# Splitting the weights of a hybrid decoder step: the low parts are computed on VectorE instead of GpSimd

## The chip, the cores and the metric

The kernel runs on one core of a Trainium2 chip. Five engines work side by side, each through its own queue in the order in which the program stands there: TensorE (PE in the profile) multiplies matrices, VectorE (DVE) and ScalarE (ACT) work elementwise and can read TensorE's results in PSUM, GpSimd (POOL) works elementwise on SBUF, and SyncE (SP) issues the DMAs. Semaphores make one engine wait for another. The metric is the device time of one execution in microseconds. The kernel before takes 4083.31 us (median of 3 runs, 4079.41 to 4086.87).

## The reference

One layer of a decoder is computed for a prompt of 2048 tokens and for 8 sample rows with a paged cache, all in float32, with a model width of 1024. Cut to what matters:

```python
h = rmsnorm(x, g_norm1) * (1 + sc1) + sh1            # sc, sh, ga: silu(c) @ w_ada + b_ada
qkv, z, beta, a, aq, ak, av, iq, ik, iw = split(h @ w_in)
o_gdn = gated_delta_rule(silu(conv(qkv)), beta, a)   # 4 heads, in chunks
o_att = sparse_attention(aq, ak, av, iq, ik, iw)     # scores, best 256 keys of each row, softmax
x = x + ga1 * (concat(o_gdn, o_att) @ w_out)
h2 = rmsnorm(x, g_norm2) * (1 + sc2) + sh2
gate, up = split(h2 @ w_ffn_in)                      # 2 x 2816 columns
x = x + ga2 * ((silu(gate) * up) @ w_ffn_out)
```

The sample rows go through the same layer with their own cache and state.

## The kernel before

The dense products keep float32 accuracy by splitting: an operand is rounded to a high part, and the rounding error is a low part. Each dense product is three matmuls (`mm3`, lines 157 to 159): high by high, high by low, low by high. Every tile of weights (128 x 512) is made by `weights`: a DMA brings the raw tile into `wr` (two buffers), ScalarE writes the high part into `wi` (line 141, `wi` has three buffers), and line 142 writes the low part, `wr` minus the high part, on GpSimd. 712 tiles are made so. The tiles of `w_in` are stored back to DRAM the first time and reloaded whole for later groups (line 135), so that they are split once. The kernel's activations are split in the same manner, with the low part on GpSimd (lines 361, 1362 and 1425).

The prompt is worked in four groups of 512 tokens. Stage one is, for each group, the projection (`project`, a convolution and a rotary step behind it) and the DeltaNet chunks (`chunks`, `state`), with the modulation products of `w_ada` (`modulate`) between them. GpSimd does much of a chunk: the squares and the normalising of q and k (lines 745 and 752), decays (774, 776), the start of the triangular inverse (792, 793), the square root by a power (190); in the projection it does the rotary step (610 to 613) and the low part of the index queries (690). Stage two is `groups`: for each group the sparse attention of the blocks of the next group (`index`, `select`, `attend`), then `ffn`: output projection, norm, and eleven pairs of feed-forward columns, two at a time, each followed by its part of the second product, whose result is added to the residual by a multiply on VectorE (line 1352) and an add on GpSimd (1353). VectorE carries the attention: it weights and sums the index scores (1241 to 1245), finds the 256 best keys by a bisection (`select`; line 1139 counts over the whole row, ten times a block), and takes the row maxima of the logits (1280). The sample rows' attention (`sample_steps`, with `sample_gdn` inside) stands in the program ahead of the third group's `ffn` (groups are counted from nought: `ffn(2)`), the schedule puts most of it at that `ffn`'s end, and the last group, `ffn(3)`, runs alone behind it.

No order is written by hand. The tile framework schedules the whole program by a model of the engines' times, and the static order of every queue is what that schedule gives; attention and feed-forward of stage two come out interleaved. Another engine for one line therefore changes the order on all queues.

Of the kernel before, what the change touches and what calls it, by code (L numbers as in the profile page):

```python
# [24 lines left out]
F32 = mybir.dt.float32  # L25
# [4 lines left out]
OP = mybir.AluOpType  # L30
# [77 lines left out]
class K:  # L108
# [21 lines left out]
    def weights(self, src, key=None):  # L130

        nc = self.nc
        w = self.wp.tile([128, 2, 512], F32R, name="wi", tag="wi", bufs=WI)
        if key in self.kept:
            nc.sync.dma_start(w.bitcast(F32), self.kept[key])
            return w[:, 0], w[:, 1]
        wr = self.wp.tile([128, 512], F32, name="wr", tag="wr", bufs=WR)
        n = 512 // len(src)
        for j, s in enumerate(src):
            nc.sync.dma_start(wr[:, j * n:(j + 1) * n], s)  # L140
        nc.scalar.copy(w[:, 0], wr)  # L141
        nc.gpsimd.tensor_tensor(w[:, 1], wr, w[:, 0].bitcast(F32), op=OP.subtract)  # L142
        if key is not None:
            self.kept[key] = self.dr.tile([128, 2, 512], F32, name="kept")
            nc.sync.dma_start(self.kept[key], w.bitcast(F32))
        return w[:, 0], w[:, 1]
# [1347 lines left out]
```

## Time and profile before

| | before |
|---|---|
| median of 3 runs | 4083.31 us |
| profiled execution | 4080.21 us, span 4078.1 us |
| TensorE busy | 3699.3 us (91%) |
| GpSimd busy | 1992.0 us (49%) |
| VectorE busy | 1873.0 us (46%) |
| ScalarE busy | 1357.3 us (33%) |
| granted TensorE clock, mean | 0.952 |

Busy time is the time in which an engine executes; a group of instructions is named by its line in the kernel, its engine, what it writes and what it reads. The waits say which instruction ended an idle time of the engine named first. A granted clock of 1.0 is 2.4 GHz.

### The profile page before, as it was taken

Reading aid. Unit: us, or ns where it says so; the run is one execution under the profiler, and the core shown is the slowest. Engines: PE = TensorE matmul, PEld = TensorE weight load, DVE = VectorE, ACT = ScalarE, POOL = GpSimd, SP = SyncE. Lnnn points to the kernel's source line nnn. Section 1 sums busy time; section 2 is a strip of 40 time slices with the busy share of each in tenths; the row PEclk is TensorE's granted clock in tenths of the full one; section 3 lists DMA queues with packets and bytes.
Section 4 is the critical chain, followed back from the end, with each engine's and each line's share of the span. In section 5 each row is a group of like instructions: output and inputs, shape, how many; then the busy total and the mean of one; then the engine's idle time right before and its main releaser. Section 6 shows DMA issues by size and latency. Waiting matters only on the chain. (4 is left out here: it accounts for less than half of the span.)

```text
span 4078.1 us, 51174 instructions
## 1 busy us (share of the span) xinstructions
PE 3699.3 (91%) x17420; PEld 2852.2 (70%) x17420; DVE 1873.0 (46%) x3492; ACT 1357.3 (33%) x2583; POOL 1992.0 (49%) x1897
## 2 busy tenths in 40 slices
PE   8888988899798879999998999998999996889997
PEld 4766877777686657677776777876877754467775
DVE  2423432441355223866668757387671238022123
ACT  2233223322332333333344443344433331132222
POOL 3366234432621575544564555564555552246555
PEclk9899999999899889999999999999999996989998
DMA  6653453373346334355535333234333333332222
GB/s 233 209 204 118 128 199 113 118 239 132 124 157 215 103 94 139 101 145 163 154 105 172 92 95 102 88 119 162 93 103 101 91 101 126 133 100 81 80 78 71
DMA packets 368313, 528.21 MB, mean 130 GB/s; under 512 B 45612, under 2 KB 246353, under 8 KB 365986
## 3 DMA queue, kind: packets, MB, share of 16 engines
q1 hardware_dynamic: 368042, 524.86, 40.5%
q8 instruction: 139, 2.28, 0.2%
q14 instruction: 132, 1.08, 0.1%
HBM read 427.33 MB, written 116.36 MB: 133 GB/s over the span
## 5 line engine op out<-in xcount | busy, mean ns | idle before, releaser
L142 POOL TENSOR_TENSOR wi<-wr,wi 128x512 fp32r<-128x512 f32 x712 | 937.6, 1323 | 1060.3 <-ACT wi L141 1030.7
L141 ACT CAST wi<-wr 128x512 fp32r<-128x512 f32 x712 | 439.5, 620 | 1118.7 <-PE d L159 345.6
L157 PE MATMUL d<-hh,wi 128*128 128x512 f32 x1792 | 736.0, 411 | 23.4 <-DVE tm L1352 7.0
L158 PE MATMUL d<-hl,wi 128*128 128x512 f32 x1792 | 717.2, 400 | 0.0
L159 PE MATMUL d<-hh,wi 128*128 128x512 f32 x1792 | 653.4, 403 | 0.0
L157 PEld LDWEIGHTS d<-hh,wi 128*128 128x128 f32 x1792 | 339.6, 190 | 118.9 <-DVE tm L1352 11.3
L159 PEld LDWEIGHTS d<-hh,wi 128*128 128x128 f32 x1792 | 338.3, 189 | 89.1 <-issue 6.7
L158 PEld LDWEIGHTS d<-hl,wi 128*128 128x128 f32 x1792 | 339.5, 189 | 77.5 <-issue 5.5
L1353 POOL TENSOR_TENSOR xt<-xt,tm 128x512 f32<-128x512 f32 x224 | 302.4, 1366 | 50.5 <-DVE tm L1352 34.3
L157 PE MATMUL d<-wi,hh 128*128 128x512 f32 x768 | 297.2, 411 | 24.5 <-DMA wi<-kept 15.5
L1245 DVE SCALAR_TENSOR_TENSOR sc<-rl,iw,sc 128x512 f32<-128x512 f32 (+3 forms) x224 | 222.2, 992 | 196.3 <-ACT rl L1238 187.4
L158 PE MATMUL d<-wi,hh 128*128 128x512 f32 x768 | 308.9, 402 | 0.2 <-POOL wi L142 0.2
L159 PE MATMUL d<-wi,hl 128*128 128x512 f32 x768 | 306.0, 400 | 0.0
L158 PE MATMUL d<-wi,ah 128*128 128x512 f32 x704 | 275.9, 395 | 0.9 <-POOL wi L142 0.9
L159 PE MATMUL d<-wi,al 128*128 128x512 f32 x704 | 271.4, 397 | 0.0
L157 PE MATMUL d<-wi,ah 128*128 128x512 f32 x704 | 256.5, 407 | 7.6 <-ACT ah L1424 3.6
L1352 DVE TENSOR_TENSOR tm<-d,row 128x512 f32<-128x512 f32 x224 | 150.1, 685 | 221.9 <-PE d L159 160.4
L1419 DVE SCALAR_TENSOR_TENSOR th<-th,d 128x512 f32<-128x512 f32 x88 | 58.1, 682 | 373.5 <-ACT th L1418 373.3
L806 DVE COPY_PREDICATED Dm<-cl,g 128x512 f32<-128x512 uint8 x96 | 70.0, 731 | 312.0 <-PE g L805 311.8
L1238 ACT ACTIVATE rl<-s 128x512 f32<-128x512 f32 (+3 forms) x288 | 148.1, 543 | 149.2 <-PE s L1236 110.4
L1139 DVE TENSOR_SCALAR_CACHE_REDUCE bias<-sc,sv 128x640 bf16<-128x640 f32 (+11 forms) x120 | 193.3, 1611 | 3.2
L157 PEld LDWEIGHTS d<-wi,hh 128*128 128x128 f32 x768 | 146.5, 192 | 66.4 <-DMA wi<-kept 17.8
(504 smaller groups left out, 6398.7 us busy)
## 6 DMA issues: line engine op xcount, KB each, us to landing
wr<-in_w_ffn_in_dram SPq DMA_DIRECT2D x704, 128.0 KB, 2.3
wi<-kept SPq DMA_DIRECT2D x168, 512.0 KB, 4.1
wr<-in_w_ffn_out_dram SPq DMA_DIRECT2D x176, 256.0 KB, 2.7
kept<-wi SPq DMA_DIRECT2D x56, 512.0 KB, 2.9
xt<-in_x_prompt_dram SPq DMA_DIRECT2D x8, 2048.0 KB, 7.6
wr<-in_w_ada_dram SPq DMA_DIRECT2D x64, 256.0 KB, 2.8
wr<-in_w_out_dram SPq DMA_DIRECT2D x64, 256.0 KB, 2.6
wr<-in_w_in_dram SPq DMA_DIRECT2D x56, 256.0 KB, 3.7
```

The lines of the kernel that those rows point to most:

```text
L141: nc.scalar.copy(w[:, 0], wr)
L142: nc.gpsimd.tensor_tensor(w[:, 1], wr, w[:, 0].bitcast(F32), op=OP.subtract)
L157: nc.tensor.matmul(out, wh, xh, start=start, stop=False, **kw)
L158: nc.tensor.matmul(out, wh, xl, start=False, stop=False, **kw)
L159: nc.tensor.matmul(out, wl, xh, start=False, stop=stop, **kw)
L806: nc.vector.copy_predicated(v4(Dm), self.cl[:, lv, :].unsqueeze(1).to_broadcast([128, H, 128]), v4(pp))
L1139: nc.vector.tensor_scalar(c, s, t, None, op0=OP.is_ge, op1=OP.add, accum_out=cnt)
L1238: nc.scalar.activation(r[:, :w], ps[:, :w], AF.Relu)
L1245: nc.vector.scalar_tensor_tensor(s, r[:, :w], iw, s, op0=OP.mult, op1=OP.add)
L1352: nc.vector.tensor_tensor(tm[:rows], pd[:rows], rw, op=OP.mult)
L1353: nc.gpsimd.tensor_tensor(xt, xt, tm[:rows], op=OP.add)
L1419: nc.vector.scalar_tensor_tensor(th, th, 1.0, pd[j], op0=OP.add, op1=OP.mult)
```

## The change

```diff
         nc.scalar.copy(w[:, 0], wr)
-        nc.gpsimd.tensor_tensor(w[:, 1], wr, w[:, 0].bitcast(F32), op=OP.subtract)
+        nc.vector.tensor_tensor(w[:, 1], wr, w[:, 0].bitcast(F32), op=OP.subtract)
```

The 712 subtractions of line 142 go from GpSimd's queue to VectorE's. Everything else computes what it did, where it did; its place in the queues is found anew by the scheduler. Three places show how.

GpSimd's queue where the last group's DeltaNet chunks meet the modulation products (`Y`, `S`, `kq`, `rnz`, `qk`, `qe` and `kd` belong to the chunks). Before:

```order
589 L855 TENSOR_TENSOR Y<-qe 128x512
590 L142 TENSOR_TENSOR wi<-wr,wi 128x512
591 L849 TENSOR_TENSOR S_169<-S_170,gc 128x512
592 L745 TENSOR_TENSOR kq<-qk 128x1024
593 L142 TENSOR_TENSOR wi<-wr,wi 128x512
594 L190 TENSOR_TENSOR r4z<-r4y,mhalf 128x4
595 L142 TENSOR_TENSOR wi<-wr,wi 128x512
596 L190 TENSOR_TENSOR rnz<-rny,mhalf 128x8
597 L859 TENSOR_TENSOR qe<-qe,r4z 128x512
598 L142 TENSOR_TENSOR wi<-wr,wi 128x512
599 L752 TENSOR_TENSOR qk<-qk,rnz 128x1024
```

The same place now:

```order
547 L855 TENSOR_TENSOR Y<-qe 128x512
548 L849 TENSOR_TENSOR S_169<-S_170,gc 128x512
549 L745 TENSOR_TENSOR kq<-qk 128x1024
550 L190 TENSOR_TENSOR r4z<-r4y,mhalf 128x4
551 L859 TENSOR_TENSOR qe<-qe,r4z 128x512
552 L190 TENSOR_TENSOR rnz<-rny,mhalf 128x8
553 L860 TENSOR_TENSOR qe<-qe,gzc 128x512
554 L752 TENSOR_TENSOR qk<-qk,rnz 128x1024
```

The chunks' own instructions follow each other, without a weight tile between them.

VectorE's queue in the bisection of a block of the second group (`bias` and `sv` are the mask and the small values of `select`, `big` the logits). Before:

```order
1213 L1139 TENSOR_SCALAR bias,sv<-sc,sv 128x1024
1214 L1140 TENSOR_SCALAR sv<-sv 128x1
1215 L1141 SCALAR_TENSOR_TENSOR sv<-sv,sW 128x1
1216 L1139 TENSOR_SCALAR bias,sv<-sc,sv 128x1024
1217 L1280 ISA big,st<-s,bias,st 128x384
1218 L1280 ISA st 128x1
1219 L1140 TENSOR_SCALAR sv<-sv 128x1
```

Now, in the bisection of the same block:

```order
1422 L1139 TENSOR_SCALAR bias,sv<-sc,sv 128x1024
1423 L1140 TENSOR_SCALAR sv<-sv 128x1
1424 L142 TENSOR_TENSOR wi<-wr,wi 128x512
1425 L1141 SCALAR_TENSOR_TENSOR sv<-sv,sW 128x1
1426 L1280 ISA big,st<-s,bias,st 128x384
1427 L1280 ISA st 128x1
1428 L1139 TENSOR_SCALAR bias,sv<-sc,sv 128x1024
```

A weight tile's low part now waits in one queue with the counts of the bisection and the logits' maxima.

TensorE's queue where the sample rows' attention follows `ffn(2)`: line 1035 transposes the paged index keys of one sample row, 1039 and 1041 score them, 908 opens `sample_gdn`. Before, the last two rows' steps and what stands behind them:

```order
9678 L159 MATMUL d<-wi,al 128x512
9679 L1039 MATMUL g<-big,iqTs 8x512
9680 L1322 MATMUL d<-cf,mod 128x128 x4
9681 L1039 MATMUL g<-big,iqTs 8x512
9682 L1322 MATMUL d<-cf,mod 128x128 x4
9683 L1041 MATMUL s<-big,oT 8x512
9684 L908 MATMUL g<-cf,big 128x24 x12
9685 L1333 MATMUL d<-cf,mod 8x128 x4
9686 L1041 MATMUL s<-big,oT 8x512
9687 L913 MATMUL g<-cf,raws 8x128 x8
9688 L1333 MATMUL d<-cf,mod 8x128 x4
9689 L157 MATMUL d<-wi,hh 128x512
```

Now the same place:

```order
9759 L1035 MATMUL g<-cf,PT 64x128 x4
9760 L1041 MATMUL s<-big,oT 8x512
9761 L1035 MATMUL g<-cf,PT 64x128 x4
9762 L1039 MATMUL g<-big,iqTs 8x512 x2
9763 L1041 MATMUL s<-big,oT 8x512
9764 L908 MATMUL g<-cf,big 128x24 x12
9765 L1041 MATMUL s<-big,oT 8x512
9766 L913 MATMUL g<-cf,raws 8x128 x12
9767 L929 MATMUL g<-rl,ones 128x64
```

Before, dense matmuls (line 157, the first of the last group's output projection) stand between and behind these steps; now the index steps of four and a half of the eight sample rows stand behind the last dense matmul, and `sample_gdn` follows them directly.

## Rows read from the trace of the kernel before

**Rows 1.** The page: busy time, share of the span and instructions of each engine.

```profile
PE 3699.3 (91%) x17420; PEld 2852.2 (70%) x17420; DVE 1873.0 (46%) x3492; ACT 1357.3 (33%) x2583; POOL 1992.0 (49%) x1897
```

**Rows 2.** Windows, four stages: start:end, length, busy us by engine, clock, DMA share, GB/s.

```profile
0.00:1561.00 1561.00, 1358.57 (x7253) 1090.64 (x7253) 556.42 (x1220) 473.37 (x951) 676.39 (x846) 0.93 0.48 157
1561.00:3105.00 1544.00, 1468.77 (x6449) 1145.52 (x6448) 1034.05 (x1806) 612.66 (x1132) 828.34 (x632) 0.98 0.40 123
3105.00:3540.00 435.00, 386.39 (x1633) 250.58 (x1632) 147.11 (x271) 118.20 (x209) 171.05 (x164) 0.90 0.35 113
3540.00:4078.10 538.10, 485.55 (x2091) 365.44 (x2089) 135.41 (x197) 153.11 (x292) 316.21 (x259) 0.96 0.27 82
```

**Rows 3.** The same windows for line 142 alone: GpSimd busy, clock, DMA share, GB/s.

```profile
0.00:1561.00 1561.00, 179.19 (x139) 0.93 0.48 157
1561.00:3105.00 1544.00, 495.11 (x369) 0.98 0.40 123
...
3540.00:4078.10 538.10, 182.83 (x143) 0.96 0.27 82
```

**Rows 4.** What TensorE waited for, whole run: us in total, times, longest.

```profile
PE d L694 <- POOL iqs L690: 27.0, 6, 6.8
PE d L174 <- POOL wi L142: 19.6, 15, 2.9
...
PE g L729 <- POOL qk L752: 16.4, 9, 5.1
...
PE g L729 <- POOL E L793: 9.1, 5, 4.8
```

**Rows 5.** Windows: a stretch of chunks with modulation products, all engines; columns as in Rows 2.

```profile
1423.00:1488.00 65.00, 41.62 (x192) 26.66 (x190) 18.42 (x44) 21.90 (x38) 59.88 (x50) 0.79 0.35 102
```

**Rows 6.** The same stretch, line 142 alone.

```profile
1423.00:1488.00 65.00, 26.04 (x22) 0.79 0.35 102
```

**Rows 7.** Groups of instructions, shapes apart: busy us, mean ns | idle before, releasers.

```profile
L142 POOL TENSOR_TENSOR wi<-wr,wi 128x512 fp32r<-128x512 f32 x712 | 937.6, 1323 | 1060.3 <-ACT wi L141 1030.7 <-DMA wr<-in_w_ffn_in_dram 7.8 <-DMA kept<-wi 5.8
...
L1245 DVE SCALAR_TENSOR_TENSOR sc<-rl,iw,sc 128x512 f32<-128x512 f32 x167 | 176.2, 1055 | 155.3 <-ACT rl L1238 149.2 <-ACT ah L1424 0.5
```

**Rows 8.** Lines 629, 1352 and 1245: duration ns min/median/max, first and last start, forms.

```profile
L629 DVE SCALAR_TENSOR_TENSOR cth<-cth,ca x48: 623/684/707, 100.8 to 1236.9; 128x512 f32<-128x512 f32 x48
...
L1352 DVE TENSOR_TENSOR tm<-d,row x224: 666/685/693, 1526.6 to 4053.6; 128x512 f32<-128x512 f32 x112
...
L1245 DVE SCALAR_TENSOR_TENSOR sc<-rl,iw,sc x224: 336/753/1868, 1630.6 to 2955.7; 128x512 f32<-128x512 f32 x85, 128x128 f32<-128x128 f32 x9, 128x256 f32<-128x256 f32 x9, 128x384 f32<-128x384 f32 x9
```

**Rows 9.** Windows of stage two, each about a pair of feed-forward steps; columns as in Rows 2.

```profile
1688.00:1781.00 93.00, 85.07 (x364) 66.99 (x363) 68.03 (x159) 33.92 (x66) 46.15 (x37) 0.95 0.40 113
...
2196.00:2328.00 132.00, 121.24 (x522) 90.59 (x521) 108.78 (x199) 56.24 (x107) 64.04 (x49) 0.97 0.39 123
...
2511.00:2599.00 88.00, 87.95 (x390) 70.15 (x390) 42.48 (x63) 36.08 (x63) 48.00 (x37) 1.00 0.31 93
...
2798.00:2930.00 132.00, 124.09 (x540) 94.88 (x541) 102.37 (x171) 57.90 (x108) 60.69 (x46) 0.96 0.38 120
2930.00:3021.00 91.00, 89.41 (x384) 69.63 (x383) 75.43 (x113) 32.23 (x53) 50.01 (x39) 1.00 0.31 91
```

**Rows 10.** Timeline of TensorE behind ffn(2): start us, us, instruction [idle before <-releaser].

```profile
3345.22 0.92 PE L908 MATMUL g<-cf,big 24*128 24x24 f32 x12
...
3359.04 0.40 PE L159 MATMUL d<-wi,hl 128*128 128x512 f32 x1
...
3432.00 1.09 PE L1064 MATMUL g<-cf,big 128*128 128x128 f32 x4 [2.44 <-DMA big<-kp_d]
```

**Rows 11.** Timeline of VectorE in the same stretch.

```profile
3361.67 4.85 DVE L1470 SCALAR_TENSOR_TENSOR xt<-xt,fin4z,row 128x1024 f32<-128x1024 f32 x4
```

**Rows 12.** The chain that ended last, at its end: start us, us, what.

```profile
4045.18 1.25 POOL wi L142
4046.44 1.26 POOL xt L1353
```

## Prediction

> **What bounds the kernel now.** I read the page's busy shares first [rows 1]: TensorE is busy 91% of the span, VectorE 46%, GpSimd 49%. The kernel is TensorE's as long as the others deliver in time; the change moves work between two engines that are half idle on the average. The average hides stages, so the next view is the table of windows. I cut the span into four stages [rows 2]: stage one (projections, DeltaNet chunks, modulation), stage two (feed-forward with the attention of the blocks to come), stage three (the end of ffn(2) and the sample rows), stage four (ffn(3) alone). In stage one TensorE is busy 1358.6 of 1561 us, 87%, with VectorE at 36% and GpSimd at 43%. In stage two it is at 95%, with VectorE at 67% and GpSimd at 54%. In stage three it is at 89%. In stage four it is at 90% as a whole, with VectorE at 25%; the loss lies at the ends of that stage. So stage one has VectorE to spare, and stage two is the place where VectorE is already the fuller of the two.
>
> The same windows for line 142 alone say where the moved work lies [rows 3]: 139 of the 712 subtractions in stage one (179.2 us of GpSimd), 369 in stage two (495.1 us), 143 in stage four (182.8 us), and by difference about 61 in stage three.
>
> The third view is the list of waits of TensorE [rows 4]. GpSimd ends 27.0 us of its waits with the index queries (line 690), 19.6 with line 142, 16.4 with the normalised q and k (752), 9.1 with the start of the inverse (793): 72 us, nearly all in stage one. The window 1423 to 1488 shows why [rows 5]: GpSimd is busy 59.9 of 65 us, TensorE only 41.6 at a granted clock of 0.79. Of the 59.9 us, 26.0 are line 142 [rows 6].
>
> **The change part by part.** 712 subtractions of 1323 ns each leave GpSimd, 937.6 us [rows 7]; GpSimd keeps 1054 us. VectorE gets 712 instructions that no row of before shows on it in this form. The nearest row is line 629, the same size with both inputs in SBUF: median 684 ns, at most 707 [rows 8]. The other end is line 1245, also two inputs in SBUF, which takes 1055 ns at this size in stage two [rows 7], with single ones up to 1868 ns, while line 1352, with one input from PSUM, never leaves 666 to 693 ns [rows 8]. The difference is company: line 1245 runs while GpSimd is 54% busy, and what is 128x512 from two SBUF inputs there costs 1055 - 684 = 371 ns more. So I bound one subtraction by 0.68 and 1.06 us. With line 142 gone GpSimd is busy (828.3 - 495.1) / 1544 = 22% of stage two. If the surcharge goes with GpSimd's share, it becomes 371 x 22/54 = 150 ns: I take 0.83 us for one subtraction, and line 1245 gains 0.22 us in each of its 224, 49 us.
>
> This has a rule behind it. The Trainium skill, page SBUF — State Buffer, section Who interferes with whom, says that a VectorE instruction with two SBUF inputs and a GpSimd instruction that reads SBUF exclude each other, and that the second to come waits for the whole of the first. The trace agrees: line 1245 against line 1352 above. It speaks against this change, since the subtraction keeps two SBUF inputs and only changes sides. By the rule a surcharge stays as long as GpSimd reads SBUF beside it, and the sum is the one below; without it a subtraction would take 0.68 us, line 1245 would lose its whole 371 ns (83 us), and VectorE would stand at (1034 + 252 - 83) / 1544 = 78% in stage two.
>
> Stage one. Line 142's own 19.6 us of TensorE's waits shrink to a third, since the queue is emptier and the instruction shorter: 13 us gained. The other 52.5 us are chains of GpSimd work in which line 142 has 179.2 of 676.4 us, 26%: 14 us gained. In the other direction 139 x 0.75 = 104 us come onto VectorE, which then stands at 42% of the stage; that cover is ample. I take -27 us; the bounds are 0, if other links of these chains are as late, and -72, if all these waits go. The order shows GpSimd's queue there without the tiles, so the relief itself is certain.
>
> Stage two. VectorE gets 369 x 0.83 = 306 us and loses 49: 1034 + 306 - 49 = 1291 of 1544 us, 84% instead of 67%, 17 points more in every window. In single windows [rows 9] that is 73 + 17 = 90% (from 1688), 82 + 17 = 99% (2196), 78 + 17 = 95% (2798), 83 + 17 = 100% (2930), but 48 + 17 = 65% (2511). Cut at the pairs of feed-forward steps, stage two has fifteen such windows, and nine of them, 985 us together, have VectorE at 67% or more now, 75% on the average, with TensorE busy 933 us of them, 95%. Rows 9 show how TensorE fares with VectorE's load: 99.9% at 48, and 91 to 98% at 73 to 83. An engine that works in order at 92% or more can't be on time for each tile. What waits: a subtraction now stands behind counts of the bisection and logits' maxima, and waits for ScalarE's high part, as GpSimd did for 1030.7 us in all [rows 7]; behind it the attention's next instructions stand, and TensorE needs both, the tile for the feed-forward and the scores' sums for the attention. The cover is two finished tiles ahead. I take 90% for TensorE in the nine windows: 933 / 0.90 = 1037, which is 52 us more. The bounds: 0, if the schedule's interleaving holds and the cover is enough; and with 1.06 us each and no gain for line 1245 the load grows by 25 points to 100% in the nine windows, and with a tenth of the time lost between instructions they take 985 / 0.90 = 1094, which is 110 us more.
>
> Stage three. The schedule, which sees a fuller VectorE, moves the attention back against the feed-forward; in TensorE's order the index steps of four and a half of the eight sample rows now stand behind the last dense matmul. Before, `sample_gdn` begins at 3345.22 and the dense matmuls run on to 3359.04 beside it [rows 10]: these 13.8 us of the chain to the paged keys (3432.00) are no longer covered. The four final scalings of 4.85 us that stand in that chain on VectorE [rows 11] now stand ahead of it: -5. The sample steps themselves are TensorE's work that was done elsewhere before, but alone each waits about 1 us for ScalarE: +4. The sum is +13; the bounds are -5 (only the scalings count) and +35 (the steps take 5 us each and nothing comes back).
>
> Stage four. VectorE goes from 25% to (135.4 + 143 x 0.83) / 538 = 47%, which is still cover for every tile. Off the last chain goes one subtraction of 1.25 us that stood between two adds on GpSimd [rows 12]: -2, between 0 and -8.
>
> The sum: -27 + 52 + 13 - 2 = +36 us on the profiled execution's 4080.2 us, 4116. That execution lies 3 us below the median of the runs, so I forecast 4119 us.
>
> **The rivals.** *GpSimd's relief decides (faster).* In stage two the schedule knows the new load and has put the subtractions between the counts one by one; if no tile comes more than two tiles late, TensorE keeps its 95% and the 52 us are nought. It decides from the point at which stage two and three together lose less than the 27 us of stage one. With -45 in stage one (half-way to its bound), +5 in stage three and -2 in stage four it is -42: 4041. For it: VectorE has 16% left in stage two and much more elsewhere, and at 83% (window 2930) TensorE was still busy 98%. Against it: no window of before has VectorE over 83%, and four would have it at 90% or more among those shown. The Trainium skill, page GPSIMD Engine Reference, section 4.1 Engine selection, sends elementwise work on two inputs to VectorE as the faster engine; by that rule the 4041 would be the outcome, and rows 7 and 8 agree as to the single instruction, 1323 against 684 ns.
>
> *The two cancel (no change).* Stage one's gain and stage two's loss are both a few tens of us from bounds that include 0; with -27, +20, +10 and -2 the time stays: 4084. For it: TensorE has 91% of the span already. Against it: it needs two unlike sizes to meet.
>
> *The exclusion costs full price (much slower).* If each subtraction meets an instruction of GpSimd as line 1245 did, it takes 1.06 us and GpSimd's adds are held as well: +110 in stage two, +13, and -15 in stage one: +108, 4191. For it: single ones of 1868 ns. Against it: GpSimd is 22% busy then, not 54%.
>
> **How the numbers follow.** The forecast 0.50, with 4090 to 4155 as its own range; GpSimd's relief 0.24; no change 0.13; full price 0.13. I count as no change what lies within 0.2% (8 us), about what a measurement of this kernel can tell. Slower: 0.50 + 0.13 = 0.63; same 0.13; faster 0.24. The range 4045 to 4185 leaves out about half of the relief's chance and half of the full price's.
>
> **What would show it.** In the profile after, GpSimd should stand near 1050 us and VectorE near 1873 + 712 x 0.83 - 49 = 2415 us. Line 142 on VectorE should take 0.75 to 0.9 us on the mean, line 1245 at 128x512 about 0.83. Stage one should end some 27 us earlier, with the waits for lines 690, 752 and 142 smaller; stage two should be some 50 us longer with TensorE below 93%, its new waits ending with VectorE (line 142, 1280, 1245). Behind ffn(2) the sample steps should stand alone. I am wrong if TensorE keeps 95% in stage two, or if stage one gains more than stages two and three lose.

## The result and the profile after

The changed kernel takes 4036.29 us (median of 4 runs, 4033.40 to 4039.23), the kernel before 4081.36 us beside it (4 runs): the ratio is 0.9889, with a 95% interval of 0.9872 to 0.9906. The forecast was 4119 us, slower; the kernel became 45 us faster, and lies 9 us below the lower end of the range. The profiled execution took 4033.4 us, its span is 4031.2.

The page's busy shares of the kernel after, to be read beside [rows 1]:

```profile
PE 3688.9 (92%) x17420; PEld 2836.7 (70%) x17420; DVE 2266.7 (56%) x4204; ACT 1360.0 (34%) x2583; POOL 1103.1 (27%) x1185
```

GpSimd lost the 712 instructions. VectorE gained only 394 us of busy time, although the subtractions alone keep it busy 546.1 us, as the groups of instructions show (shapes apart; busy us, mean ns, then the idle time before):

```profile
L142 DVE TENSOR_TENSOR wi<-wr,wi 128x512 fp32r<-128x512 f32 x712 | 546.1, 771 | 731.5 <-ACT wi L141 726.9 <-DMA wr<-in_w_ada_dram 2.3 <-PE d L174 0.5
...
L1245 DVE SCALAR_TENSOR_TENSOR sc<-rl,iw,sc 128x512 f32<-128x512 f32 x167 | 148.0, 886 | 43.7 <-ACT rl L1238 38.0
```

So by busy time everything else on VectorE adds 1873.0 + 546.1 - 2266.7 = 152 us less than before. Of these, 46 us are only overlap: the records of line 142 overlap those of its neighbours. Without the records of line 142 VectorE is busy 1766 us, 107 less than before, and that is the work which became shorter. Line 1245 went from 1055 to 886 ns at this size [rows 7]; it is not alone, as the last section shows. GpSimd lost less than the 938 us of line 142: 1992.0 - 1103.1 = 889 us. What stays there became longer, above all the adds of line 1353, from 302.4 to 326.2 us.

The same four stages as windows of the kernel after, cut at the same pieces of work as [rows 2] (start:end, length, busy us of TensorE, its weight loads, VectorE, ScalarE, GpSimd, then clock, DMA share, GB/s):

```profile
0.00:1514.00 1514.00, 1330.09 (x7177) 1066.93 (x7177) 648.88 (x1354) 471.04 (x946) 516.55 (x708) 0.95 0.49 162
1514.00:3035.00 1521.00, 1459.04 (x6460) 1141.74 (x6461) 1189.45 (x2168) 609.10 (x1126) 353.33 (x262) 0.99 0.40 123
3035.00:3495.00 460.00, 411.94 (x1689) 261.52 (x1688) 194.03 (x344) 125.17 (x220) 90.16 (x101) 0.86 0.35 110
3495.00:4031.20 536.20, 487.87 (x2097) 366.52 (x2096) 234.32 (x340) 154.64 (x293) 143.04 (x116) 0.96 0.27 83
```

Two columns tell the story: the length, and the length less TensorE's busy time, its idle time.

| stage | length before, after | difference | predicted | idle before, after |
|---|---|---|---|---|
| one | 1561, 1514 | -47 | -27 | 202, 184 |
| two | 1544, 1521 | -23 | +52 | 75, 62 |
| three | 435, 460 | +25 | +13 | 49, 48 |
| four | 538, 536 | -2 | -2 | 53, 48 |

TensorE's idle time fell in every stage (in stage three by half a microsecond), by 37 us in all; its busy time fell by 10. The lengths of the stages alone mislead, since the schedule also hands work from one to the next, and the granted clock changes. Stage three's 25 us are no idle time: by an estimate from these rows 13 us are 56 more matmuls at the 237 ns of before, and 12 us are slower matmuls (244 ns on the mean, with the granted clock at 0.86 instead of 0.90).

TensorE's waits, to be read beside [rows 4]:

```profile
PE d L694 <- POOL iqs L690: 24.0, 7, 6.8
...
PE d L174 <- DVE wi L142: 13.2, 20, 1.9
...
PE g L729 <- POOL E L793: 8.8, 2, 6.1
PE g L729 <- POOL qk L752: 8.2, 5, 3.2
```

The four together fell from 72 to 54 us, about as much as stage one's idle time. Other waits changed there too and cancel: in stage one, all waits that end with GpSimd fell from 84 to 57 us and those that end with ScalarE from 42 to 34, while those that end with VectorE, now with line 142 among them, rose from 53 to 68. The stretch of DeltaNet chunks and modulation products that stood in [rows 5], at the same place of the kernel after:

```profile
1396.00:1461.00 65.00, 50.36 (x266) 35.45 (x265) 43.82 (x78) 28.04 (x49) 38.08 (x28) 0.89 0.43 129
```

GpSimd is busy 38 instead of 60 us there, TensorE 50 instead of 42, and the granted clock is 0.89 instead of 0.79.

The seven stretches of stage two in which VectorE is fullest, cut at the pairs of feed-forward steps as in [rows 9]:

```profile
1626.00:1717.00 91.00, 84.35 (x370) 65.93 (x370) 82.90 (x197) 30.61 (x60) 17.42 (x14) 1.00 0.41 116
2007.00:2133.00 126.00, 114.19 (x484) 87.31 (x482) 109.10 (x199) 52.38 (x104) 38.98 (x29) 0.96 0.43 137
2133.00:2252.00 119.00, 113.96 (x510) 88.43 (x509) 107.05 (x199) 59.23 (x113) 28.93 (x24) 0.97 0.39 127
2435.00:2527.00 92.00, 90.95 (x394) 69.95 (x393) 80.29 (x143) 29.14 (x53) 19.83 (x13) 1.00 0.33 99
2660.00:2732.00 72.00, 68.36 (x303) 51.42 (x301) 68.18 (x123) 32.03 (x61) 13.20 (x11) 1.00 0.45 148
2732.00:2852.00 120.00, 113.79 (x501) 87.66 (x502) 107.68 (x182) 52.65 (x99) 29.46 (x22) 0.99 0.39 125
2944.00:3035.00 91.00, 90.00 (x382) 68.39 (x381) 85.36 (x149) 29.68 (x48) 17.24 (x14) 1.00 0.33 101
```

Over these 711 us VectorE is busy 641 us, 90%, and TensorE 676, 95%. The prediction had put TensorE at 90% in such windows.

Behind ffn(2), the timelines of TensorE and of VectorE, to be read beside [rows 10] and [rows 11]; the first row is the last dense matmul:

```profile
3274.90 0.40 PE L159 MATMUL d<-wi,hl 128*128 128x512 f32 x1
...
3307.89 1.47 PE L908 MATMUL g<-cf,big 24*128 24x24 f32 x12
...
3386.12 1.09 PE L1064 MATMUL g<-cf,big 128*128 128x128 f32 x4 [2.63 <-DVE sc L1117]
```

```profile
3273.24 4.87 DVE L1470 SCALAR_TENSOR_TENSOR xt<-xt,fin4z,row 128x1024 f32<-128x1024 f32 x4 [1.13 <-POOL fin4z L190]
```

As predicted, the last rows' index steps stand alone between the dense matmuls and `sample_gdn` (line 908), and the final scalings stand ahead of it; from line 908 to line 1064 it takes 78 instead of 87 us. What was not predicted is the clock. These windows show the index steps and the stretch behind them, first in the kernel before, then in the kernel after:

```profile
3249.00:3347.00 98.00, 98.00 (x391) 53.73 (x390) 15.24 (x25) 36.86 (x67) 56.09 (x45) 1.00 0.31 91
...
3356.00:3432.00 76.00, 41.31 (x186) 37.60 (x184) 71.01 (x126) 1.41 (x6) 26.90 (x11) 0.54 0.35 115
```

```profile
3284.00:3396.00 112.00, 76.10 (x254) 44.59 (x253) 85.73 (x153) 8.66 (x16) 24.32 (x10) 0.50 0.27 83
```

Before, the index steps run between dense matmuls at a granted clock of 1.00, and the low clock comes behind them, in `sample_gdn`. Now they run behind the last dense matmul, and 9 us after it, at 3284, the granted clock falls to 0.50, which is 1.2 GHz. It stays there for 112 us. Four matmuls of line 1039 took 1.88 us before and take 3.58 us there.

### The profile page after: what moved, and what is told of

It reads as the page before. It is cut to its first block, busy times and chain, and to the rows that moved or that the text cites. A ratio compares the mean times of both kernels' runs of the same rounds, so it can differ in the third digit from the quotient of the medians.

```text
span 4031.2 us, 51014 instructions
## 1 busy us (share of the span) xinstructions
PE 3688.9 (92%) x17420; PEld 2836.7 (70%) x17420; DVE 2266.7 (56%) x4204; ACT 1360.0 (34%) x2583; POOL 1103.1 (27%) x1185
## 4 chain that ended last, share of the span: by engine, by line
PE 66%; DVE 12%; DMA 8%; issue 5%; POOL 4%; ACT 4%; SPq 1%; ACTq 0%; DVEq 0%; POOLq 0%
PE d L157 15%; PE d L158 15%; PE d L159 15%; PE g L1304 2%; DVE wi L142 2%; PE s L1236 2%; PE s L1279 2%; PE g L800 2%; PE g L805 2%; DMA wr<-in_w_ada_dram 1%; DMA wi<-kept 1%; PE g L729 1%; PE g L1298 1%; DMA wr<-in_w_ffn_in_dram 1%; ACT wi L141 1%
## 5 line engine op out<-in xcount | busy, mean ns | idle before, releaser
L142 DVE TENSOR_TENSOR wi<-wr,wi 128x512 fp32r<-128x512 f32 x712 | 546.1, 771 | 731.5 <-ACT wi L141 726.9
L1353 POOL TENSOR_TENSOR xt<-xt,tm 128x512 f32<-128x512 f32 x224 | 326.2, 1477 | 546.1 <-DVE tm L1352 455.8
L1425 POOL TENSOR_TENSOR al<-ca,ah 128x512 fp32r<-128x512 f32 x88 | 121.1, 1391 | 1002.9 <-ACT ah L1424 977.4
L157 PE MATMUL d<-wi,ah 128*128 128x512 f32 x704 | 264.6, 413 | 22.7 <-DVE tm L1352 12.7
L158 PE MATMUL d<-wi,ah 128*128 128x512 f32 x704 | 280.9, 401 | 0.3 <-DVE wi L142 0.2
L1245 DVE SCALAR_TENSOR_TENSOR sc<-rl,iw,sc 128x512 f32<-128x512 f32 (+3 forms) x224 | 185.0, 826 | 56.9 <-ACT rl L1238 48.5
L157 PEld LDWEIGHTS d<-wi,ah 128*128 128x128 f32 x704 | 131.9, 189 | 67.8 <-DVE tm L1352 16.0
```

The source lines that it names most:

```text
L142: nc.vector.tensor_tensor(w[:, 1], wr, w[:, 0].bitcast(F32), op=OP.subtract)
L157: nc.tensor.matmul(out, wh, xh, start=start, stop=False, **kw)
L158: nc.tensor.matmul(out, wh, xl, start=False, stop=False, **kw)
L1245: nc.vector.scalar_tensor_tensor(s, r[:, :w], iw, s, op0=OP.mult, op1=OP.add)
L1353: nc.gpsimd.tensor_tensor(xt, xt, tm[:rows], op=OP.add)
L1425: nc.gpsimd.tensor_tensor(al[b], a, ah[b].bitcast(F32), op=OP.subtract)
```

## The experiments

Three questions: to what does stage one's gain belong, why did stage two not lose, and how full may VectorE become? Each kernel was timed beside the kernel before. The table cuts each profile at the end of stage one (behind a set of four residual multiplies, line 1352, of the first output projection) and gives length, TensorE's busy time and its idle time of both parts, from windows like those above (us). In the texts on record, "139 tiles" of stage one and 573 (once 576) behind it were counted by time; by the program it is 120 and 592, since 19 tiles of the first output projection are made before stage one has ended.

| kernel | ratio to before, 95% | stage one: length, busy, idle | behind it: length, busy, idle |
|---|---|---|---|
| before | 1 | 1561, 1359, 202 | 2517, 2341, 176 |
| after | 0.9889 (0.9872 to 0.9906) | 1514, 1330, 184 | 2517, 2359, 158 |
| e1_stage1 | 0.9934 (0.9919 to 0.9948) | 1513, 1328, 185 | 2539, 2358, 181 |
| e2_ffn | 0.9986 (0.9977 to 0.9995) | 1561, 1361, 200 | 2518, 2347, 171 |
| e3_idle_sub | 1.0020 (1.0006 to 1.0033) | 1563, 1364, 199 | 2532, 2352, 180 |
| e12_memset | 1.0018 (1.0004 to 1.0032) | 1569, 1361, 208 | 2518, 2349, 170 |
| e10_ada | 0.9939 (0.9919 to 0.9959) | 1529, 1334, 195 | 2527, 2356, 171 |
| e4_twice | 1.0271 (1.0254 to 1.0289) | 1601, 1377, 224 | 2592, 2379, 213 |
| e7_idle_vec | 0.9946 (0.9924 to 0.9967) | 1515, 1331, 185 | 2546, 2364, 181 |
| e8_twice_ffn | 1.0052 (1.0032 to 1.0071) | 1519, 1335, 185 | 2583, 2379, 204 |
| e5_wi2_after | 1.0046 (1.0032 to 1.0060) | 1639, 1398, 241 | 2458, 2313, 145 |
| e6_wi2_before | 1.0193 (1.0169 to 1.0217) | 1674, 1417, 257 | 2487, 2326, 160 |
| e9_chain | 0.9811 (0.9792 to 0.9830) | 1485, 1325, 160 | 2516, 2354, 162 |
| e11_more | 0.9804 (0.9788 to 0.9821) | 1485, 1335, 150 | 2520, 2351, 169 |

**One half at a time.** A flag tells the stages apart:

```diff
-        nc.gpsimd.tensor_tensor(w[:, 1], wr, w[:, 0].bitcast(F32), op=OP.subtract)
+        (nc.vector if self.stage == 1 else nc.gpsimd).tensor_tensor(...)   # e1_stage1
+        (nc.gpsimd if self.stage == 1 else nc.vector).tensor_tensor(...)   # e2_ffn
```

Expected of e1_stage1:

> The subtractions of stage one alone (139 of 712 tiles: projections and modulation) are on VectorE, those of the feed-forward groups stay on GpSimd as before. Theory 'relief' (the gain comes from GpSimd's queue in stage one, where its own chains hold up TensorE): nearly all of the 45 us come, 4036 to 4050 us, and stage one is about 40 us shorter than before. Rival 'short tile' (each tile is ready sooner because its subtraction takes 0.69 instead of 1.29 us): 139/712 of the 45 us, 9 us, so about 4072 us. Rival 'new order' (the schedule's other interleaving gives it, whatever the engines' load): no reason for stage one in particular, anything from 4040 to 4085 us.

Expected of e2_ffn:

> The reverse: stage one's subtractions on GpSimd as before, those of the output projection and feed-forward (576 of 712) on VectorE. 'Relief': little is left, 4065 to 4085 us; stage one as long as before (1561 us up to the first residual adds), stage two some 20 us shorter and stage three some 25 us longer, as in the changed kernel. 'Short tile': 80% of the gain, 36 us, about 4045 us.

Measured: 4054.34 us with stage one's tiles alone, 4077.38 with all others alone. The two parts of e1_stage1, then of e2_ffn, as windows:

```profile
0.00:1513.30 1513.30, 1328.34 (x7170) 1065.34 (x7171) 634.08 (x1333) 470.07 (x945) 534.58 (x725) 0.95 0.49 162
1513.30:4052.50 2539.20, 2357.76 (x10253) 1771.15 (x10250) 1333.24 (x2280) 889.07 (x1638) 1311.19 (x1053) 0.96 0.36 111
```

```profile
0.00:1561.00 1561.00, 1361.43 (x7250) 1091.38 (x7251) 570.22 (x1238) 473.90 (x951) 652.85 (x827) 0.93 0.48 157
1561.00:4079.30 2518.30, 2346.83 (x10173) 1763.85 (x10170) 1620.04 (x2848) 885.55 (x1632) 584.58 (x479) 0.96 0.36 112
```

Stage one's gain belongs wholly to its own tiles: e1_stage1 has all 48 us of it, e2_ffn none. Its total still missed the 4036 to 4050 expected of it, by 4 us, since behind stage one it took 22 us longer than the kernel before. The other tiles cost nothing behind it. By TensorE's idle time they saved a little there: 5 us against the kernel before (e2_ffn), 23 us as the second half of the change (from e1_stage1 to after). That the two differ suggests how much a new schedule moves by itself, some 10 to 20 us. In stage one a chance of the order is not the cause: the runs fall into two groups although each has an order of its own, with 1513 to 1519 us where GpSimd is relieved (e1_stage1, after, e7_idle_vec, e8_twice_ffn) and 1561 to 1569 us where it is loaded (before, e2_ffn, and e3_idle_sub and e12_memset below).

**Which of GpSimd's queue and the shorter tile.** Idle work loads GpSimd again behind every tile while the tile stays on VectorE (`idle` is a scratch tile of 160 columns without a reader, made as `self.wp.tile([128, 160], F32, ...)`):

```diff
         nc.vector.tensor_tensor(w[:, 1], wr, w[:, 0].bitcast(F32), op=OP.subtract)
+        for c, n in ((0, 160), (160, 160), (320, 64)):                       # e3_idle_sub
+            nc.gpsimd.tensor_tensor(idle[:, :n], hi[:, c:c + n], hi[:, c:c + n], op=OP.subtract)
+        for c in range(6): nc.gpsimd.memset(idle, 0.0)                       # e12_memset
```

(`hi` stands for the high part, `w[:, 0]`.) Expected of e3_idle_sub:

> The changed kernel, and for each tile GpSimd also makes three subtractions (160, 160 and 64 columns, high part minus itself, about 1.3 us together) whose result nobody reads: GpSimd is as loaded as before, but no tile waits for it. 'Relief': the gain goes, 4070 us or more (VectorE has its load too, and the two engines exclude each other on SBUF), stage one back to about 1555 us. 'Short tile': the gain stays, 4036 to 4050 us. 'New order': the order is another again, no forecast.

Expected of e12_memset:

> The changed kernel with six memsets of 160 columns into a scratch tile on GpSimd behind every weight tile (an estimate of 1.3 us for the six, from memsets of this size in the trace, 0.22 us each). They read no SBUF and no weight tile waits for them. With idle subtractions, which read SBUF, GpSimd was busy 724 instead of 517 us in stage one, and stage one's gain of 47 us was gone. Theory Q (the place in GpSimd's queue is what counts): stage one loses most of it again, 1545 or more, 4070 to 4090. Rival S (reading SBUF beside VectorE is what counts): stage one stays within 12 us of 1514, and VectorE's lines 1245 and 1141 are as short as in the changed kernel; 4036 to 4050.

Measured: 4091.08 and 4091.27 us. Stage one of e3_idle_sub, then of e12_memset:

```profile
0.00:1562.60 1562.60, 1363.83 (x7315) 1097.06 (x7316) 666.75 (x1368) 476.33 (x955) 723.60 (x1121) 0.93 0.48 157
```

```profile
0.00:1569.10 1569.10, 1361.01 (x7271) 1091.80 (x7272) 659.99 (x1361) 474.37 (x952) 1292.45 (x4177) 0.93 0.47 157
```

With GpSimd loaded as before (724 us against 676 [rows 2]) stage one is as long as before, with the tile made on VectorE all the same. TensorE's waits that end with GpSimd stand at 73 us in this stage, against 57 in the kernel after and 84 in the kernel before. So the relief of GpSimd is the cause, and the shorter subtraction by itself is not. The idle subtractions do more than fill the queue: they read the finished tile and so hold its buffer, and ScalarE waits 38 us for them in stage one before it writes a next high part. The memsets hold no weight tile and read nothing. They take the gain away as well, while VectorE's busy time stays within some 11 us of the 649 of the kernel after: GpSimd's load alone can do it. One thing went otherwise than planned: the memsets wait for nothing, so many ran ahead, and GpSimd is busy 776 us more in stage one than in the kernel after, instead of the estimated 180. Against reading SBUF the memsets are thus no equal dose, and they don't show how much a microsecond of the queue costs. Nor do they show the way to TensorE: its waits that end with GpSimd stay at 55 us there, and those that end with VectorE grow from 68 to 96, while VectorE's own waits for GpSimd grow from 61 to 81. That fits chains which pass through both engines; what part the new order has in it is not shown. Stage one is as long as theory Q expected, and the total lies 1 us above its range.

**Where in stage one.** In the kernel before, only those tiles of stage one that aren't kept for a reload (the 64 of the modulation products) go to VectorE:

```diff
+        (nc.vector if self.stage == 1 and key is None else nc.gpsimd).tensor_tensor(...)
```

> The kernel before, with only stage one's tiles that are not kept (the modulation products' tiles) on VectorE; the tiles of w_in stay on GpSimd, as do all of the feed-forward. With all 139 tiles of stage one on VectorE stage one fell from 1561 to 1513 us. My theory (GpSimd's queue is late where DeltaNet chunks and modulation products share it, as in the stretch 1423 to 1488 of the kernel before): 25 to 40 of the 48 us belong to these tiles; stage one 1521 to 1536, about 4060. Rival (the first projection, which makes its tiles under TensorE's eyes, has most of it): at most 15 us, stage one 1546 or more, about 4075.

Measured: 4058.68 us, stage one 1529 us. These 64 tiles give 32 of the 48 us, and by difference the other 56 (of `w_in`, in the first projection) 16. So two thirds of the gain belong to tiles that are made as in the stretch which the prediction chose in [rows 5].

**VectorE's load: made fuller.** All subtractions twice (e4_twice), or twice from stage two on (e8_twice_ffn), or with idle subtractions from stage two on, for which no tile waits (e7_idle_vec):

```diff
         nc.vector.tensor_tensor(w[:, 1], wr, w[:, 0].bitcast(F32), op=OP.subtract)
+        nc.vector.tensor_tensor(w[:, 1], ...)                                # e4_twice
+        if self.stage == 2: nc.vector.tensor_tensor(w[:, 1], ...)            # e8_twice_ffn
+        if self.stage == 2: (160 + 160 + 64 columns, hi minus hi, into idle, on VectorE)   # e7_idle_vec
```

Expected of e4_twice:

> The changed kernel with every subtraction made twice on VectorE: 712 x 0.77 = 546 us more there, 2810 us in all, about 96% of stage two. It prices the crowding of VectorE that the prediction put at 52 us for 84%. If crowding is cheap as long as the schedule knows of it: under 30 us more than the changed kernel, below 4066 us. If it bites near the full engine: 80 us or more, above 4115 us, nearly all of it in stage two.

Expected of e7_idle_vec:

> The changed kernel, with three subtractions without a reader added on VectorE behind every weight tile of stage two and of what follows (573 tiles; 160, 160 and 64 columns, together the 384 columns, into a scratch tile). No weight tile waits for them; stage one is as in the changed kernel. VectorE's load in stage two rises by about as much as in the run with every subtraction made twice (it stood at 1430 of 1664 us there, and stage two was 142 us longer than in the changed kernel). Theory L (load: what counts is how full VectorE's queue is): stage two 80 us or more longer than the changed kernel's 1521, all in all 4120 to 4200. Theory T (the tile's own delay: the tile must come later to hurt): stage two at most 30 us longer, 4040 to 4075.

Expected of e8_twice_ffn:

> The changed kernel, with the subtraction made twice on VectorE for the 573 tiles of stage two and of what follows, and once in stage one. The second one stands in the tile's own path. It is the partner of the run with idle work on VectorE. If both lose alike, the load decides; if this one alone loses, the tile's delay. From the run with all 712 made twice (stage one +87, stage two +142 against the changed kernel) I expect stage one within 20 us of 1514, stage two about 1640 to 1665, and 4110 to 4150 in all; if stage two's loss in that run came from a later stage one, less than 60 us is left here.

Measured: 4194.67, 4061.62 and 4103.96 us. Stage two of e4_twice, of e7_idle_vec (with six crowded stretches) and of e8_twice_ffn:

```profile
1601.00:3265.50 1664.50, 1541.06 (x6604) 1173.95 (x6603) 1430.05 (x2577) 636.29 (x1165) 357.14 (x280) 0.97 0.38 116
```

```profile
1515.00:3146.00 1631.00, 1526.16 (x6678) 1175.85 (x6679) 1463.87 (x3322) 633.55 (x1162) 345.83 (x280) 0.98 0.38 118
...
1626.00:1720.00 94.00, 83.26 (x352) 61.70 (x350) 89.76 (x259) 30.69 (x60) 16.10 (x12) 1.00 0.38 107
...
1930.00:2030.00 100.00, 94.36 (x413) 73.28 (x412) 92.17 (x227) 37.09 (x69) 16.00 (x13) 1.00 0.43 128
2030.00:2130.00 100.00, 87.87 (x390) 67.02 (x388) 97.84 (x218) 41.88 (x85) 34.40 (x25) 1.00 0.45 149
2130.00:2230.00 100.00, 91.45 (x399) 67.32 (x398) 97.58 (x228) 49.90 (x97) 18.95 (x16) 0.95 0.39 129
2230.00:2330.00 100.00, 96.38 (x406) 72.84 (x404) 98.32 (x223) 35.96 (x62) 18.86 (x15) 1.00 0.33 101
...
2730.00:2830.00 100.00, 83.05 (x329) 59.56 (x328) 95.23 (x203) 40.98 (x86) 23.76 (x18) 0.93 0.46 151
```

```profile
1519.30:3172.50 1653.20, 1538.31 (x6703) 1178.39 (x6701) 1431.51 (x2589) 636.46 (x1168) 365.90 (x280) 0.98 0.38 117
```

In e7_idle_vec VectorE is busy 1464 of 1631 us, 90% of the whole stage, more than the 84% that the prediction feared, and TensorE still 93.6%. Stage two is 110 us longer than in the kernel after, but that is mostly work which the schedule brought forward from stage three (218 more matmuls); everything behind stage one is 29 us longer, 23 of them idle. In single stretches TensorE gets 96% beside a VectorE at 98%, and 83% beside one at 95%: VectorE's share alone doesn't tell. Yet it counts: cut into sixteen stretches, stage two has five with VectorE at 95% or more, with TensorE at 89% (442 of 494 us), and nine with VectorE at 84 to 94%, with TensorE at 95% (866 of 910 us). In e8_twice_ffn VectorE is less full, 87%, and the loss behind stage one is 66 us, 45 of them idle. The difference between the two edits is that in e8_twice_ffn the tile itself comes later. The expectation for e8_twice_ffn held for stage one and two (1519 and 1653 us) and missed the total by 6 us. My expectation for theory L, stage two 80 us or more longer, was met in the letter and missed in the total that it was to stand for: 4120 at least was expected, 4062 measured. Theory T's total holds (4040 to 4075), its 30 us hold for everything behind stage one, not for stage two alone. The idle subtractions are not quite free for the tiles either: they too hold the tile's buffer until they have read it, and ScalarE waits 192 us in all for line 142 there, against 3 in the kernel after. TensorE lost little even so. e4_twice lost more than the 80 us expected if crowding bites, but not nearly all of it in stage two: it loses 75 us behind stage one and 87 in stage one, although VectorE is at 48% there.

**The cover.** Two buffers of finished tiles instead of three, after (e5_wi2_after) and before (e6_wi2_before):

```diff
-WR, WI = 2, 3
+WR, WI = 2, 2
```

> The changed kernel with two instead of three buffers for finished weight tiles (wi); everything else is as in the changed kernel. It asks whether the tiles made ahead are what lets a VectorE that is 78% busy in stage two (1189 of 1521 us) deliver on time. Theory A (cover decides): with one tile less ahead, a tile that waits in VectorE's queue behind counts and maxima is late for TensorE; TensorE's idle time before line 157's matmuls that ends with line 142 or 141 grows from 13 + 12 us to over 60, stage two becomes at least 50 us longer, and the time is about 4110 (over 4085). Theory B (the schedule places the subtractions early enough, cover hardly used): all stages within 20 us of the changed kernel, 4036 to 4060.

> The kernel before (low parts on GpSimd) with two instead of three buffers for finished weight tiles. It is the partner of the changed kernel with two buffers, which lost 65 us, all of it in stage one (1639 us long instead of 1514), and nothing behind it. Theory A (the third tile is what hides the making of a tile in stage one, and the making is longer on GpSimd, 1.32 against 0.69 us): stage one loses more than there, 140 us or more, and some 30 us behind it; about 4230. Theory B (with two buffers the pace is set by the reloads and the DMAs, not by the engine of the low part): stage one loses 100 to 130 us as there, nothing behind it; about 4160.

Measured: 4101.54 and 4162.12 us. The two parts of e5_wi2_after, then of e6_wi2_before:

```profile
0.00:1638.90 1638.90, 1398.27 (x7446) 1111.30 (x7446) 675.85 (x1460) 493.13 (x992) 516.43 (x721) 0.93 0.47 154
1638.90:4096.90 2458.00, 2312.52 (x9974) 1714.49 (x9974) 1552.85 (x2746) 865.32 (x1593) 564.43 (x464) 0.97 0.36 112
```

```profile
0.00:1674.10 1674.10, 1417.49 (x7452) 1117.22 (x7453) 620.31 (x1364) 493.69 (x991) 691.16 (x860) 0.92 0.46 151
1674.10:4160.60 2486.50, 2326.31 (x9969) 1725.80 (x9967) 1251.06 (x2130) 864.12 (x1593) 1296.87 (x1037) 0.97 0.36 111
```

The third buffer is worth 65 us after and 79 before. All the idle time that its loss costs lies in stage one (57 and 54 us there); behind stage one TensorE's idle time even falls by 13 and 16 us. So neither theory of the first run held as written. Theory A's time was met (4102, over 4085), and stage two, which ends at 3257 us there, is 97 us longer. But that is work handed on, 328 more matmuls, and its idle time grows by 7 us only: stage two's punctuality doesn't come from the third tile. Theory B's 4036 to 4060 was missed. Theory B of the second run held, 4160 expected.

**Further on the same way.** More of GpSimd's stage-one chains go to VectorE: the index queries' low part (690), the squares and normalising of q and k (745, 752), the start of the inverse (792, 793); then (e11_more) also 361, 754, 757, 774, 776, 859 and 860:

```diff
-        nc.gpsimd.tensor_tensor(qk8, qk8, col(rn), op=OP.mult)
+        nc.vector.tensor_tensor(qk8, qk8, col(rn), op=OP.mult)        # 752; the other lines alike
```

> The changed kernel, and also on VectorE: the low part of the index queries (line 690, 32 instructions of 0.73 us on GpSimd), the squares and the normalising of q and k in a chunk (lines 745 and 752, 16 each of 1.9 us) and the start of the triangular inverse (792 and 793, 16 each of 1.27 us). All of it is stage one; GpSimd's busy time falls by about 125 us there. Theory R (GpSimd's chains are what TensorE waits for in stage one: 24.0 us for line 690, 8.2 for 752, 8.8 for 793 in the changed kernel): stage one ends 15 to 40 us earlier than 1514, the rest is the same within 20 us, 3995 to 4025. Rival (the chain moves to VectorE's queue, which carries the convolution and the evictions there): nothing or a loss, 4036 to 4060, with new waits of TensorE that end with VectorE's lines 745 to 793.

> The changed kernel with the index queries' low part and the chunks' squares, normalising and start of the inverse on VectorE (4004 us), and beyond that: the low part of the normalised activations (line 361, 64 of 1.37 us on GpSimd), the decays (774, 776), the scaled q and k (754, 757) and the output's normalising and gating (859, 860), 16 each of 1.1 to 1.4 us. VectorE would stand at about 55% of stage one. Theory (GpSimd's chains were TensorE's waits, and after the last run hardly any wait is left that ends with GpSimd: lines 613, 860 and 754 make 13 us): 0 to 15 us faster than 4004. Rival (VectorE's queue becomes the late one, its lines 752, 806 and 690 already end 38 us of waits): 5 to 30 us slower than 4004, and GpSimd's share was not worth lowering further.

Measured: 4003.83 us (4002.49 to 4011.23) and 4004.43 us (4002.65 to 4007.15). e9_chain beats both kernels: 0.9811 of before (0.9792 to 0.9830), some 32 us below the changed kernel. Its two parts, and what is left of TensorE's waits for the moved lines:

```profile
0.00:1484.80 1484.80, 1324.87 (x7177) 1063.08 (x7177) 707.95 (x1449) 470.44 (x946) 407.67 (x611) 0.96 0.50 165
1484.80:4001.00 2516.20, 2353.77 (x10245) 1767.11 (x10243) 1614.14 (x2853) 888.84 (x1638) 587.65 (x478) 0.96 0.36 112
```

```profile
PE g L729 <- DVE qk L752: 14.1, 4, 7.7
...
PE d L694 <- DVE iqs L690: 11.4, 11, 2.4
```

Stage one is 29 us shorter and the rest as it was. Line 690's waits halve, line 793's 8.8 us shrink, line 752's grow: the chain now stands in VectorE's queue, and is still the better for it. e11_more adds nothing in time. Its stage one has 10 us less idle time and 10 us more busy time, with 71 more matmuls in it; hardly any wait was left to take from GpSimd, as expected.

## Why the prediction was wrong

- **The failed step** is "I take 90% for TensorE in the nine windows", +52 us, with the sentence before it: "An engine that works in order at 92% or more can't be on time for each tile." TensorE stood at 95% in the fullest windows of the kernel after, beside a VectorE at 90%, and at 95% too in the fullest of them, where VectorE has 94.7% (68.18 of 72 us). Stage two became 23 us shorter. At 90% over the whole stage (e7_idle_vec) VectorE still delivered for 29 us of loss in all. The slope that I drew from [rows 9], TensorE falling from 99.9 to 91% as VectorE fills, came from five windows of one kernel. In e7_idle_vec there is a slope, but it lies higher: TensorE has 95% beside a VectorE at 84 to 94%, and 89% only in the stretches with VectorE at 95% or more. As cut above, no stretch of the kernel after is that full. The order is made anew with the new load known, and the order rows ahead of the prediction showed it: the subtractions lie between the counts one by one. I had this as the rival's argument and gave it 0.24.
- **VectorE's load** was the second error, in the same term: 2415 us and 84% of stage two forecast, 2267 us and 78% measured. The subtraction was priced well, 0.83 us forecast and 0.771 measured. What GpSimd's leaving gives back to the rest of VectorE was not: 49 us forecast, 107 us of shorter work measured and 46 us of overlap with line 142. Line 1245 gained 0.17 us at 128x512 instead of 0.22, but the relief wasn't confined to it. The low end that I had worked out as the case without the rule, 78%, came true although the subtractions still pay a surcharge. GpSimd, forecast near 1050 us, stands at 1103: that its own instructions become longer beside the subtractions was in no term.
- **The cover**, "two finished tiles ahead", was no argument either way for stage two: a buffer less adds no idle time behind stage one, and costs 65 to 79 us in all by stage one's idle time.
- **Stage one** had the right cause and place (e1, e3, e10) and was sized too small, -27 against -47. The waits fell by 18 us, less than my 27. The rest is TensorE's busy time, -28.5. By an estimate, 11 us of it are 76 fewer matmuls: they are small ones of the chunks (lines 800, 805 and 729, 0.13 to 0.16 us each) that went to the later stages. The other 18 us are shorter matmuls, as the granted clock rose from 0.93 to 0.95 [rows 2] while TensorE waited less. I had priced idle time only.
- **Stage three** had the right order: the sample steps stand alone, the scalings ahead of them. But its terms are waits, and idle time stayed at 49 and 48 us; the +4 for steps that wait for ScalarE is not there, since TensorE is busy without a gap from 3275 to 3309. The +25 instead of +13 is about half work handed on and half the granted clock, which falls to 0.50 while the steps stand alone. I had no term for it.
- **Stage four** was right, -2, and the last chain of the kernel after has no subtraction of line 142 between the adds.
- **The sum**: -47 - 23 + 25 - 2 = -47 us on the span. The rival "GpSimd's relief decides" gave 4041 and was right in its mechanism: TensorE keeps its 95% in stage two (95.9%). Its stage terms were not exact either: -45, nought, +5 and -2 stand against -47, -23, +25 and -2, so its nearness in the total is in part luck.
- **The rule on SBUF** that the prediction cites (the Trainium skill, page SBUF — State Buffer, section Who interferes with whom), that instructions of VectorE with two SBUF inputs and GpSimd's reading ones exclude each other, agrees with the rows of the last section and yet didn't speak against the change. What the subtractions still pay on VectorE (771 ns mean against 692 median) is 56 us, what GpSimd's own instructions pay beyond that is 37 us (the sum of their durations), and what VectorE's others save is 107.

Open: which part of the 10 to 20 us by which e1, e2 and the whole change differ behind stage one belongs to the engine and which to the new order. Every edit gives a new schedule, and no run held the order while it changed the engine. How GpSimd's load reaches TensorE in e12_memset is open too.

## What to carry to other kernels

Ask of an engine not how full it becomes but whether what it makes comes late: under a schedule that knows the load, an engine 90% busy delivered nearly on time, while 0.6 us more of VectorE's busy time for each tile in its own path cost more than twice as much as 0.8 us beside it (66 against 29 us). Only where it was 95% busy or more did TensorE fall to 89%. An engine at 43% can be the late one where chains of a few instructions go through it one after the other; the waits by releaser and one crowded window show it, and the busy share does not. When work leaves an engine that shares SBUF with another, count what all of the other's instructions get back, and what the instructions that stay on the other engine pay. Compare stages by TensorE's idle time, its matmuls and its granted clock, since a new schedule moves work across the marks, and here the clock fell once the small sample steps stood alone.

## What the hardware showed beyond that

GpSimd's company lengthens small instructions of VectorE far beyond their size. Lines 1430 and 1431 (8x256, two inputs in SBUF, in stage four) follow each other on VectorE while GpSimd makes the low parts of two blocks of activations (line 1425). One such passage in the kernel before, then in the kernel after, from the timelines of GpSimd and VectorE (start us, us, instruction):

```profile
3635.19 2.73 POOL L1425 TENSOR_TENSOR al<-ca,ah 128x512 fp32r<-128x512 f32 x2
...
3636.18 0.59 DVE L1430 SCALAR_TENSOR_TENSOR th<-th,fold 8x256 f32<-8x256 f32 x1 [0.48 <-ACT th L1429]
3636.81 1.40 DVE L1431 SCALAR_TENSOR_TENSOR th<-th,fold 8x256 f32<-8x256 f32 x1
```

```profile
3589.98 2.56 POOL L1425 TENSOR_TENSOR al<-ca,ah 128x512 fp32r<-128x512 f32 x2 [26.47 <-ACT ah L1424]
...
3591.70 1.12 DVE L1430 SCALAR_TENSOR_TENSOR th<-th,fold 8x256 f32<-8x256 f32 x1 [0.48 <-ACT th L1429]
3592.86 0.41 DVE L1431 SCALAR_TENSOR_TENSOR th<-th,fold 8x256 f32<-8x256 f32 x1
```

Alone such an instruction takes 0.41 us. The one that runs when GpSimd's second subtraction ends takes 1.40 or 1.12 us, and it ends 0.27 to 0.28 us behind that subtraction in all eleven passages of both kernels (3638.21 against 3637.92 here, 3592.82 against 3592.54). The change only moved the meeting: before, ten of eleven times line 1431 waits, with a median of 1397 ns; after, line 1430 waits every time (1116 ns) and line 1431 takes 411 ns. The two lines together went from 20.6 to 16.8 us. The subtraction that they meet is not line 142's but line 1425's, which stays on GpSimd in both kernels.

Line 1141, one column wide in the bisection, fell from a mean of 439 to 300 ns with the change, while its median stayed at 219: fewer are held up, 16 instead of 42 of 140 take over 0.4 us. They gave back 19 us, more than half as much as line 1245's 37 (222.2 to 185.0 us in its index scores). The group of line 1141 in the kernel before and after:

```profile
L1141 DVE SCALAR_TENSOR_TENSOR sv<-sv,sW 128x1 f32<-128x1 f32 x140 | 61.5, 439 | 3.0
```

```profile
L1141 DVE SCALAR_TENSOR_TENSOR sv<-sv,sW 128x1 f32<-128x1 f32 x140 | 42.0, 300 | 2.6
```
